# Query and key products of a hybrid GLA/RetNet trunk: three matmuls of 256 columns in two PSUM banks in place of one of 512 and one of 256 in four

## The chip, the cores and the metric

The kernel runs on one core of a Trainium2 chip. TensorE (PE in the profile) multiplies; its weight loads are listed apart, as PEld. VectorE (DVE), ScalarE (ACT) and GpSimd (POOL) do the rest, and SyncE (SP) issues most DMAs. TensorE writes its results to PSUM, eight banks of 128 x 512 float32 values. The metric is the time of one execution on the device, in microseconds (us); lower is better.

## The reference

The model has two layers over a sequence of 256 tokens with 2048 channels: a gated linear attention (GLA, 4 heads) and a retention layer (8 heads). Each normalizes its input, projects it to queries, keys, values and gates, mixes tokens with a decay, normalizes each head, multiplies by `silu(gate)`, projects back and adds the result to its input. What matters here are the projections:

```python
proj = h @ w_in                                   # h: 256 x 2048
q, k, v, gate = jnp.split(proj, [...], axis=-1)
...
return (o * jax.nn.silu(gate)) @ w_out
```

A head has 256 query and 256 key columns, so a head's queries and keys together are one block of 512 columns of `w_in`. All values are float32.

## The kernel before

**Precision.** A float32 product is made of three products of split numbers. Every weight block and every activation is split into a high part, rounded to the matmul's format, and a low part, the rest. High by high, high by low and low by high are summed in PSUM. The activations lie in `xhl`: for each of 16 rows of channel tiles (`kt`), the high and the low copy of all 256 tokens side by side, 512 columns.

**Weights.** They stream from HBM in pieces of 128 x 2 x 512 (512 KB), called subs here. `emit_split` makes a sub's high part on ScalarE (L283) and its low part on VectorE (L284). `next_weights` runs three subs ahead of TensorE (`LOOK`), with four buffers for each part. DMAs run up to six subs ahead (`DMA_LOOK`) in eight buffers. The list of subs, and so the order of loads, is made by `_plan`.

**Values and gates** have tokens as PSUM rows: the weight that TensorE holds is a tile of activations, and 512 weight columns stream past (`group_x`, `product`, `direct`). One bank holds 128 tokens. Most of these products go through a scheme with seven products in place of eight (Strassen's kind) over half of the channels: `P1` to `P8` are half products over summed activations or summed weights, `v4` to `g7` are plain steps. Weight sums are made partly by DMAs that add into a loaded piece (`emit_split`, L292, on GpSimd's queue) and partly on VectorE (L278). `values_and_gates` works through a string of such tokens with four banks, A, B, C and V1: A and B end as the gates, C and V1 as the values. `UNIT` is the order of a GLA pair, `WHOLE` that of retention heads 0 and 4 (eight q/k steps first), and `MIXED` that of the other six retention heads, in which q/k steps stand between the products.

**Queries and keys** have channels as PSUM rows, since the scores need them so: TensorE holds a 128 x 128 tile of weights, and tokens stream past. `step_w` does this for one sub: 2 rows of tiles (`q`) by 4 column blocks (`c`). For each, the high weights meet high and low tokens in one matmul of 512 columns, which fills a whole bank (`ps[c]`, half for high tokens, half for low), and the low weights meet the high tokens in one of 256 columns, which adds to the first half. A head has eight such steps, and four banks for its four column blocks: two of the ring of four (`acc`), and two of the pool `lev`; GLA head 0 has four of the ring. At the end the two halves of each bank are added: ScalarE copies the second half out, and VectorE adds the first (`evac_w` for GLA, `qk_done` for retention).

**Order.** `acc` hands the ring's banks out in turn, unless it is told which. Small work of a head (rotary angles, scores, norms, transposes) is a generator that advances by one step after each token (`advance`, `step`, `turn`). In `ret_head`, `drain` names the token at which all of the last head's small work must be done and that of this head is queued. Within these dependencies a scheduler sets each engine's final order.

Of the kernel before, what the change touches and what calls it, by code (L numbers as in the profile page):

```python
# [10 lines left out]
F32 = mybir.dt.float32  # L11
# [3 lines left out]
AF = mybir.ActivationFunctionType  # L15
ALU = mybir.AluOpType

P = 128
SEQ = 256
D = 2048  # L20
EPS = 1e-6
NKT = D // P
GW = 512
SUB = 2
NSUB = NKT // SUB
# [113 lines left out]


UNIT = "P1 v4 z P3 v5 P5 v6 P6 P2 v7 P7 g4 g5 P8 g6 g7"
MIXED = "q0 q1 P1 q2 q3 q4 z P5 q5 P6 q6 q7 P2 P3 v4 v5 v6 P7 v7 g4 g5 P8 g6 g7"
WHOLE = " ".join(f"q{j}" for j in range(NSUB)) + " " + UNIT


# [16 lines left out]
def kernel(  # L162
# [17 lines left out]
    nc = tc.nc  # L180
# [9 lines left out]
    t4_p = pool("t4", 4)  # L190
# [150 lines left out]

    def step_w(rhs, ps, j, given=True, early=False):
        hi, lo = next_weights()
        last = j == NSUB - 1
        order = [(q, c) for q in range(SUB) for c in range(4)]
        if last or (j == 0 and given):
            order = [(q, c) for c in range(4) for q in range(SUB)]
        if early:
            for q in range(SUB):
                kt = j * SUB + q  # L350
                for c in range(4):
                    keep(mm(ps[c], hi[:, q, c * P : (c + 1) * P], rhs[:, kt, :, :], start=kt == 0, stop=False))
                for c in range(4):
                    keep(mm(ps[c][:, 0, :], lo[:, q, c * P : (c + 1) * P], rhs[:, kt, 0, :], start=False, stop=False))
            order = []
        for q, c in order:
            kt = j * SUB + q
            wh = hi[:, q, c * P : (c + 1) * P]
            wl = lo[:, q, c * P : (c + 1) * P]
            if kt == NKT - 1:  # L360
                mm(ps[c][:, 0, :], wl, rhs[:, kt, 0, :], start=False, stop=False)
                mm(ps[c], wh, rhs[:, kt, :, :], start=False, stop=True)
            else:
                mm(ps[c], wh, rhs[:, kt, :, :], start=kt == 0, stop=False)  # L364
                mm(ps[c][:, 0, :], wl, rhs[:, kt, 0, :], start=False, stop=False)  # L365

    def group_w(rhs, name, extra=None, ps=None):
        given = ps is not None
        ps = ps or acc(4, f"{name}_ps", (P, 2, SEQ))
        for j in range(NSUB):  # L370
            step_w(rhs, ps, j, given, j < 3 and extra is not None and not given)
            if extra is not None:
                extra(j)
            advance()
        return ps

    def evac_w(ps, dst, name):
        tmp = t4_p.tile([P, 4, SEQ], F32, tag="t4", name=f"{name}_h2")
        with tc.high_priority():
            for c in range(4):  # L380
                nc.scalar.activation(tmp[:, c, :], ps[c][:, 1, :], AF.Copy)
                halves = lambda a: a.rearrange("p (z t) -> p z t", z=2)
                to = dst[:, c // 2, :].rearrange("p (z k t) -> p z k t", z=2, k=2)[:, :, c % 2, :]
                nc.vector.tensor_tensor(to, halves(ps[c][:, 0, :]), halves(tmp[:, c, :]), ALU.add)

    begun, closed = set(), set()

# [420 lines left out]
    def gla_head(h):  # L808
        hw = {}
        if h > 1:  # L810
            side.appendleft(gla_decay(h, hw))
        banks = None
        if h > 0:
            banks = acc(2, f"gqk{h}_ps", (P, 2, SEQ))
            banks += [lev_p.tile([P, 2, SEQ], F32, tag="lev", name=f"gqk{h}_ps{c}") for c in (2, 3)]
        ps = group_w(xhl, f"gqk{h}", None if h else first_group, banks)
        drain_side()

        def scores():
            yield from gla_scores(h, hw)  # L820

        qk = t4_p.tile([P, 2, 2 * SEQ], F32, tag="qk", name=f"qk{h}", bufs=1)
        evac_w(ps, qk, f"gqk{h}")
        hw["qk"] = qk
        if h == 0:
            side.append(gate_low_rank())
# [412 lines left out]
    def ret_head(h):  # L1239
        lhs = xhl  # L1240
        mixed = h % 4 != 0
        at = (2, 3, 0, 1) if h < 4 else (0, 1, 2, 3)
        q_ps = [acc(1, f"rqk{h}_ps{c}", (P, 2, SEQ), [at[c + 2]])[0] for c in range(2)]
        q_ps += [lev_p.tile([P, 2, SEQ], F32, tag="lev", name=f"rqk{h}_ps{c}") for c in (2, 3)]
        if not mixed:
            q_ps = q_ps[2:] + q_ps[:2]
        r, r2 = r2_[:, 0, :], r2_[:, 1, :]
        box = {}

        def qk_done():  # L1250
            if h == 0:
                token_norm(r2_, "n2")
                nc.vector.tensor_tensor(r2_[:, 1, :], r2_[:, 0, :], r2_[:, 0, :], ALU.mult)
            qk = t4_p.tile([P, 4, SEQ], F32, tag="qk", name=f"rqk{h}", bufs=1)
            tmp = t4_p.tile([P, 4, SEQ], F32, tag="t4", name=f"rqk{h}_h2")
            for c in range(4):
                nc.scalar.activation(tmp[:, c, :], q_ps[c][:, 1, :], AF.Copy)
                nc.vector.tensor_tensor(qk[:, c, :], q_ps[c][:, 0, :], tmp[:, c, :], ALU.add)
            box["qk"] = qk

        def q_step(j):
            step_w(lhs, q_ps, j)
            if j == NSUB - 1:
                qk_done()

        def tile_of(key, pool_, shape, dtype, name):
            def get():
                if key not in box:
                    box[key] = pool_.tile(shape, dtype, tag=key, name=name)
                return box[key]  # L1270

            return get

        v = tile_of("v", v_p, [P, 2, 2, GW], F32R, f"rv{h}")
        sg = tile_of("sg", sg_p, [P, 2, GW], F32, f"rsg{h}")
        o = tile_of("o", o_p, [P, 2, GW], F32, f"re{h}")
        order = ret_order(h)
        toks = [x for x in order.split() if x != "z"]
        drain = toks.index("P2" if mixed else "v5")

        def turn(tok):
            n = toks.index(tok)
            if n == drain:
                while tasks:
                    step()
                if mixed:
                    tasks.append(ret_tasks(h, box["qk"], r, r2, box))
            elif n < drain:
                if tok != "q7":
                    step()  # L1290
            elif mixed:
                if tok not in ("P7", "g4", "g5"):
                    step()
            elif tok == "P8":
                tasks.append(ret_tasks(h, box["qk"], r, r2, box))
            elif tok in ("g6", "g7"):
                step()

        def banks(n):
            if n not in box:  # L1300
                box[n] = acc(1, f"re{h}_ps{n}", which=[at[n]])[0]
            return box[n]

        values_and_gates(lhs, order, banks, v, sg, o, r, r2, turn, q_step)

    def values_and_gates(lhs, order, banks, v, sg, o, r, r2, turn, q_step=None):
# [5 lines left out]
        tt = nc.vector.tensor_tensor  # L1312
        copy = lambda dst, ps: nc.scalar.activation(dst, ps, AF.Copy)
        done = set()

        def v_split(t):
            sc = r2[:, t : t + 1]
# [5 lines left out]
        def g_done(t):  # L1323
# [7 lines left out]
            "P1": lambda: product(A(), plain(0, 0), stop=True),  # L1331
            "P2": lambda: product(B(), plain(4, 0)),
            "P3": lambda: product(C(), summed(0)),
            "P5": lambda: product(B(), summed(1), stop=True),
            "P6": lambda: product(A(), summed(2), stop=True),
            "P7": lambda: product(A(), summed(3), stop=True),
            "P8": lambda: product(A(), plain(4, 1)),
# [1 line left out]
        for tok in order.split():  # L1339
            kind, last = tok[0], tok[1:] == str(NSUB - 1)  # L1340
            if tok == "z":
                continue
            if kind == "q":
                q_step(int(tok[1:]))
            elif kind == "P":
                products[tok]()
            else:
                direct(lhs, (C(), V1()) if kind == "v" else (B(), A()), int(tok[1:]), stop=last)
            done.add(tok)
            if tok == "P1":  # L1350
                copy(sg()[:, 0, :], A())
            elif tok == "P5":
                copy(o()[:, 1, :], B())
                begun.discard(id(B()))
                closed.discard(id(B()))
            elif tok == "P6":
                copy(o()[:, 0, :], A())
                tt(o()[:, 0, :], o()[:, 1, :], o()[:, 0, :], ALU.subtract)
            elif tok == "P7":
                copy(sg()[:, 1, :], A())  # L1360
                tt(o()[:, 1, :], o()[:, 1, :], sg()[:, 1, :], ALU.subtract)
            if tok in ("v7", "P7"):
                if tok == "v7":
                    tt(o()[:, 0, :], C(), o()[:, 0, :], ALU.add)
                    v_split(0)
                if {"v7", "P7"} <= done:
                    tt(o()[:, 1, :], V1(), o()[:, 1, :], ALU.add)
                    v_split(1)
            if tok == "g7":
                for t in range(2):  # L1370
                    g_done(t)
            turn(tok)
# [135 lines left out]
```

## Time and profile before

| | |
|---|---|
| time, three runs | 1379.7, 1380.17, 1381.68 us (median 1380.17) |
| time of the profiled execution | 1379.47 us |
| its span, first to last instruction | 1377.6 us |
| matmul records, weight load records | 6632, 6632 |
| VectorE busy, ScalarE busy | 1079.1, 836.0 us |
| mean granted TensorE clock | 0.998 |

The profile is of one execution. A row of a group reads: line, engine, operation, output<-inputs, shapes, count, then busy time in us and the mean duration of one in ns, then idle time of the engine before them and what ended it. A row of the timeline begins with the start and the duration in us and ends with the idle time before it. Rows of a tile give shortest, median and longest duration in ns, and first and last start in us. Matmuls overlap in their pipeline, and their recorded ends are modelled. A row's mean duration of 390 ns is therefore not what one costs; the distance between starts is. A few matmul records can be missing.

### The profile page before, as it was taken

How to read it: one execution, taken by the hardware profiler on the slowest of the kernel's cores; microseconds unless marked ns; L12 is line 12 of the kernel's file. 1: busy time of each engine (PE TensorE's matmuls, PEld its weight loads, DVE VectorE, ACT ScalarE, POOL GpSimd, SP SyncE). 2: the span in 40 equal slices, each digit the busy share in tenths (PEclk: the TensorE clock that was granted, in tenths of full speed). 3: DMA queues.
4: the chain of work that ended last, by engine and by line, in shares of the span. 5: the costliest groups of instructions: out<-in, count | busy, mean ns of one | idle time of the engine just before them, and what ended most of it. 6: DMA issues, size and time to landing. Idle time of an engine off the chain costs nothing.

```text
span 1377.6 us, 18438 instructions
## 1 busy us (share of the span) xinstructions
PE 1366.5 (99%) x6632; PEld 1148.5 (83%) x6632; DVE 1079.1 (78%) x1497; ACT 836.0 (61%) x1104; POOL 131.8 (10%) x188
## 2 busy tenths in 40 slices
PE   9999999999999999999999999999999999999997
PEld 7888888888888888888888888888888888888887
DVE  6686795987878896769888888886858897888673
ACT  6576656656567747656666566655546666666452
POOL 1003020110021021001011010100101101010000
PEclk9999999999999999999999999999999999999999
DMA  9765556689658657858897878896798797879661
GB/s 359 245 182 160 172 177 187 151 250 343 204 153 265 204 175 180 314 168 247 279 317 202 256 203 247 208 310 206 184 372 238 217 271 193 256 199 327 211 191 62
DMA packets 83931, 312.94 MB, mean 227 GB/s; under 512 B 9712, under 2 KB 10736, under 8 KB 82560
## 3 DMA queue, kind: packets, MB, share of 16 engines
q1 hardware_dynamic: 67344, 242.64, 50.9%
q0 software_dynamic: 15056, 61.74, 22.6%
q10 hardware_dynamic: 1440, 7.38, 1.4%
q8 instruction: 52, 0.85, 0.2%
q14 instruction: 39, 0.32, 0.1%
HBM read 301.24 MB, written 10.49 MB: 226 GB/s over the span
## 4 chain that ended last, share of the span: by engine, by line
PE 99%; DMA 0%; DVE 0%; ACT 0%; DVEq 0%; issue 0%; SPq 0%
PE rqk_ps L364 8%; PE re_ps L392 8%; PE re_ps L391 8%; PE re_ps L393 8%; PE rqk_ps L365 4%; PE gqk_ps L364 4%; PE gg_ps L322 3%; PE gv_ps L321 3%; PE gv_ps L322 3%; PE gv_ps L323 3%; PE gg_ps L323 3%; PE gg_ps L321 3%; PE ge_ps L392 2%; PE ge_ps L393 2%; PE ge_ps L391 2%; PE gae_ps L391 2%
## 5 line engine op out<-in xcount | busy, mean ns | idle before, releaser
L284 DVE TENSOR_TENSOR lo<-raw,hi 128x1024 fp32r<-128x1024 f32 (+1 forms) x557 | 675.2, 1222 | 225.7 <-ACT hi L283 218.9
L283 ACT ACTIVATE hi<-raw 128x1024 fp32r<-128x1024 f32 (+1 forms) x557 | 584.5, 1056 | 390.8 <-PE gg_ps L323 49.0
L364 PE MATMUL rqk_ps<-xhl,hi 128*128 128x512 f32 x480 | 162.8, 397 | 0.0
L392 PE MATMUL re_ps<-lo,xhl 128*128 128x512 f32 x352 | 137.3, 390 | 0.0
L393 PE MATMUL re_ps<-hi,xhl 128*128 128x512 f32 x352 | 137.1, 390 | 0.0
L391 PE MATMUL re_ps<-hi,xhl 128*128 128x512 f32 x352 | 132.7, 391 | 0.0
L292 POOL DMA_DIRECT2D raw<-in_w_all x84 | 72.7, 867 | 530.3 <-DVE lo L284 283.8
L365 PE MATMUL rqk_ps<-xhl,lo 128*128 128x256 f32 x480 | 122.3, 280 | 0.0
L364 PEld LDWEIGHTS rqk_ps<-xhl,hi 128*128 128x128 f32 x480 | 89.5, 188 | 17.9
L365 PEld LDWEIGHTS rqk_ps<-xhl,lo 128*128 128x128 f32 x480 | 87.5, 189 | 3.4
L393 PEld LDWEIGHTS re_ps<-hi,xhl 128*128 128x128 f32 x352 | 66.1, 188 | 13.6
L391 PEld LDWEIGHTS re_ps<-hi,xhl 128*128 128x128 f32 x352 | 66.1, 188 | 13.3
L392 PEld LDWEIGHTS re_ps<-lo,xhl 128*128 128x128 f32 x352 | 66.1, 188 | 13.1
L364 PE MATMUL gqk_ps<-xhl,hi 128*128 128x512 f32 x216 | 76.5, 398 | 0.0
L322 PE MATMUL gg_ps<-lo,xhl 128*128 128x512 f32 x192 | 75.4, 393 | 0.0
L322 PE MATMUL gv_ps<-lo,xhl 128*128 128x512 f32 x192 | 75.2, 392 | 0.0
L321 PE MATMUL gv_ps<-hi,xhl 128*128 128x512 f32 x192 | 75.1, 393 | 0.0
L323 PE MATMUL gv_ps<-hi,xhl 128*128 128x512 f32 x192 | 75.0, 391 | 0.0
L323 PE MATMUL gg_ps<-hi,xhl 128*128 128x512 f32 x192 | 74.9, 390 | 0.0
L321 PE MATMUL gg_ps<-hi,xhl 128*128 128x512 f32 x192 | 74.8, 391 | 0.0
L365 PE MATMUL gqk_ps<-xhl,lo 128*128 128x256 f32 x216 | 59.0, 280 | 0.0
L801 POOL TENSOR_TENSOR s<-s,m 128x64 f32<-128x64 f32 x56 | 36.1, 676 | 232.7 <-DVE m L792 223.4
(407 smaller groups left out, 2682.5 us busy)
## 6 DMA issues: line engine op xcount, KB each, us to landing
raw<-in_w_all SPq DMA_DIRECT2D x451, 512.0 KB, 4.8
raw<-in_w_all POOLq DMA_DIRECT2D x84, 512.0 KB, 6.5
resid<-in_x_n SPq DMA_DIRECT2D x2, 1024.0 KB, 9.1
gg<-in_gn_g POOLq DMA_DIRECT2D x8, 256.0 KB, 3.9
resid_x<-resid ACTq DMA_DIRECT2D x1, 2048.0 KB, 9.1
gb<-in_gn_b POOLq DMA_DIRECT2D x8, 256.0 KB, 6.2
gb_resid<-resid_x POOLq DMA_DIRECT2D x1, 2048.0 KB, 11.8
resid_g<-gb_resid ACTq DMA_DIRECT2D x1, 2048.0 KB, 8.9
```

What stands on the lines that cost most here:

```text
L283: a = nc.scalar.activation(hi[:, sl], src[:, sl], AF.Copy)
L284: b = nc.vector.tensor_tensor(lo[:, sl], src[:, sl], hi[:, sl].bitcast(F32), ALU.subtract)
L292: nc.gpsimd.dma_start(raws[n], block(key), accum_op=ALU.add)
L321: mm(ps, xh, hi[:, q, :], start=kt == 0, stop=False)
L322: mm(ps, xh, lo[:, q, :], start=False, stop=False)
L323: mm(ps, xl, hi[:, q, :], start=False, stop=kt == NKT - 1)
L364: mm(ps[c], wh, rhs[:, kt, :, :], start=kt == 0, stop=False)
L365: mm(ps[c][:, 0, :], wl, rhs[:, kt, 0, :], start=False, stop=False)
L391: mm(ps, xh, hi[:, q, :], start=start, stop=False, **again)
L392: mm(ps, xh, lo[:, q, :], start=False, stop=False, **again)
L393: mm(ps, xl, hi[:, q, :], start=False, stop=stop, **again)
L801: nc.gpsimd.tensor_tensor(dst, dst, side_of(m[:, li, :], z), ALU.add)
```

## The change

The query and key matmuls all have 256 columns now. High weights by high tokens, high weights by low tokens and low weights by high tokens are three matmuls that add into the same 256 columns. So the sum is complete in PSUM, and a bank holds two column blocks. A head needs two banks. GLA heads take them from the ring; retention heads take both from `lev`. The evacuation is one ScalarE copy for each bank, and no VectorE add.

In retention heads the ring's banks are no longer held by queries and keys. In mixed heads, product 5 goes into bank C, the first values' bank, and product 3 adds onto it there. Product 2, which used to come after q7 since product 5 had bank B before it, now comes after q3. The values' first half then takes product 6 off with a subtraction at `v7`, and a subtraction on VectorE after `P6` is dropped. The small work of a mixed head is queued after q7, not after `P2`.

```diff
-MIXED = "q0 q1 P1 q2 q3 q4 z P5 q5 P6 q6 q7 P2 P3 v4 v5 v6 P7 v7 g4 g5 P8 g6 g7"
+MIXED = "q0 q1 P1 q2 q3 P2 q4 z P5 q5 P6 q6 q7 P3 v4 v5 v6 P7 v7 g4 g5 P8 g6 g7"
...
     def step_w(rhs, ps, j, given=True, early=False):
         hi, lo = next_weights()
-        last = j == NSUB - 1
+        at = lambda c: ps[c // 2][:, c % 2, :]
+        both = lambda c: {"skip_group_check": c % 2 == 1}
...
-            if kt == NKT - 1:
-                mm(ps[c][:, 0, :], wl, rhs[:, kt, 0, :], start=False, stop=False)
-                mm(ps[c], wh, rhs[:, kt, :, :], start=False, stop=True)
-            else:
-                mm(ps[c], wh, rhs[:, kt, :, :], start=kt == 0, stop=False)
-                mm(ps[c][:, 0, :], wl, rhs[:, kt, 0, :], start=False, stop=False)
...
+            a = [
+                lambda c=c, wh=wh, kt=kt: mm(at(c), wh, rhs[:, kt, 0, :], start=kt == 0 and c % 2 == 0, stop=False, **both(c)),
+                lambda c=c, wh=wh, kt=kt: mm(at(c), wh, rhs[:, kt, 1, :], start=False, stop=False, **both(c)),
+            ]
+            b = [lambda c=c, wl=wl, kt=kt: mm(at(c), wl, rhs[:, kt, 0, :], start=False, stop=kt == NKT - 1, **both(c))]
+            if not early:
+                for x in a + b:
+                    x()
+                continue
...
+    def group_w(rhs, name, extra=None, given=False):
+        ps = acc(2, f"{name}_ps", (P, 2, SEQ))
...
-    def evac_w(ps, dst, name):
-        tmp = t4_p.tile([P, 4, SEQ], F32, tag="t4", name=f"{name}_h2")
+    def evac_w(ps, dst):
         with tc.high_priority():
-            for c in range(4):
-                nc.scalar.activation(tmp[:, c, :], ps[c][:, 1, :], AF.Copy)
-                halves = lambda a: a.rearrange("p (z t) -> p z t", z=2)
-                to = dst[:, c // 2, :].rearrange("p (z k t) -> p z k t", z=2, k=2)[:, :, c % 2, :]
-                nc.vector.tensor_tensor(to, halves(ps[c][:, 0, :]), halves(tmp[:, c, :]), ALU.add)
+            for i in range(2):
+                to = dst[:, i, :].rearrange("p (z k t) -> p k z t", z=2, k=2)
+                nc.scalar.activation(to, ps[i].rearrange("p k (z t) -> p k z t", z=2), AF.Copy)
...
-        banks = None
-        if h > 0:
-            banks = acc(2, f"gqk{h}_ps", (P, 2, SEQ))
-            banks += [lev_p.tile([P, 2, SEQ], F32, tag="lev", name=f"gqk{h}_ps{c}") for c in (2, 3)]
-        ps = group_w(xhl, f"gqk{h}", None if h else first_group, banks)
+        ps = group_w(xhl, f"gqk{h}", None if h else first_group, h > 0)
...
-        q_ps = [acc(1, f"rqk{h}_ps{c}", (P, 2, SEQ), [at[c + 2]])[0] for c in range(2)]
-        q_ps += [lev_p.tile([P, 2, SEQ], F32, tag="lev", name=f"rqk{h}_ps{c}") for c in (2, 3)]
-        if not mixed:
-            q_ps = q_ps[2:] + q_ps[:2]
+        q_ps = [lev_p.tile([P, 2, SEQ], F32, tag="lev", name=f"rqk{h}_ps{c}") for c in range(2)]
...
-            tmp = t4_p.tile([P, 4, SEQ], F32, tag="t4", name=f"rqk{h}_h2")
-            for c in range(4):
-                nc.scalar.activation(tmp[:, c, :], q_ps[c][:, 1, :], AF.Copy)
-                nc.vector.tensor_tensor(qk[:, c, :], q_ps[c][:, 0, :], tmp[:, c, :], ALU.add)
+            for i in range(2):
+                nc.scalar.activation(qk[:, 2 * i : 2 * i + 2, :], q_ps[i], AF.Copy)
...
-        drain = toks.index("P2" if mixed else "v5")
+        drain = toks.index("q7" if mixed else "v5")
...
+        first = order.index("P5") < min(order.index("P3"), order.index("v4"))
...
-            "P5": lambda: product(B(), summed(1), stop=True),
+            "P5": lambda: product((C if first else B)(), summed(1), stop=True),
...
             elif tok == "P6":
                 copy(o()[:, 0, :], A())
-                tt(o()[:, 0, :], o()[:, 1, :], o()[:, 0, :], ALU.subtract)
+                if not first:
+                    tt(o()[:, 0, :], o()[:, 1, :], o()[:, 0, :], ALU.subtract)
...
-                    tt(o()[:, 0, :], C(), o()[:, 0, :], ALU.add)
+                    tt(o()[:, 0, :], C(), o()[:, 0, :], ALU.subtract if first else ALU.add)
```

Three places of TensorE's order show it. The first is in GLA head 1's queries and keys, in before (`gqk1_ps0` to `gqk1_ps2` are banks of a column block each; `hi41`, `lo41` are the parts of sub 41):

```order
L364 MATMUL gqk1_ps0_1304<-xhl_105,hi41_1215 128x512
L365 MATMUL gqk1_ps0_1304<-xhl_105,lo41_1216 128x256
L364 MATMUL gqk1_ps1_1305<-xhl_105,hi41_1215 128x512
L365 MATMUL gqk1_ps1_1305<-xhl_105,lo41_1216 128x256
L364 MATMUL gqk1_ps2_1306<-xhl_105,hi41_1215 128x512
L365 MATMUL gqk1_ps2_1306<-xhl_105,lo41_1216 128x256
```

and with the change (`gqk1_ps0` and `gqk1_ps1` hold two column blocks each):

```order
L355 MATMUL gqk1_ps0_1359<-xhl_105,hi41_1270 128x256
L356 MATMUL gqk1_ps0_1359<-xhl_105,hi41_1270 128x256
L358 MATMUL gqk1_ps0_1359<-xhl_105,lo41_1271 128x256
L355 MATMUL gqk1_ps1_1360<-xhl_105,hi41_1270 128x256
L356 MATMUL gqk1_ps1_1360<-xhl_105,hi41_1270 128x256
L358 MATMUL gqk1_ps1_1360<-xhl_105,lo41_1271 128x256
```

A pair of widths, 512 and 256, has become three rows of 256 into one place, the first two with the same weights.

The second place is the end of a mixed head's q steps, head 1, in before (`re1_ps10` is bank B, `re1_ps20` bank C, `sums` the summed activations):

```order
L365 MATMUL rqk1_ps3_6351<-xhl_105,lo297_6599 128x256
L361 MATMUL rqk1_ps3_6351<-xhl_105,lo297_6599 128x256
L362 MATMUL rqk1_ps3_6351<-xhl_105,hi297_6598 128x512
L392 MATMUL re1_ps10_6547<-lo298_6611,xhl_105 128x512
L393 MATMUL re1_ps10_6547<-hi298_6610,xhl_105 128x512
L391 MATMUL re1_ps10_6547<-hi298_6610,xhl_105 128x512
L392 MATMUL re1_ps10_6547<-lo298_6611,xhl_105 128x512
L393 MATMUL re1_ps10_6547<-hi298_6610,xhl_105 128x512
```

and with the change:

```order
L355 MATMUL rqk1_ps1_6624<-xhl_105,hi299_6951 128x256
L356 MATMUL rqk1_ps1_6624<-xhl_105,hi299_6951 128x256
L358 MATMUL rqk1_ps1_6624<-xhl_105,lo299_6952 128x256
L390 MATMUL re1_ps20_6887<-hi300_6963,sums_6124 128x512
L391 MATMUL re1_ps20_6887<-lo300_6964,sums_6124 128x512
L392 MATMUL re1_ps20_6887<-hi300_6963,sums_6124 128x512
L390 MATMUL re1_ps20_6887<-hi300_6963,sums_6124 128x512
L391 MATMUL re1_ps20_6887<-lo300_6964,sums_6124 128x512
```

Product 2 stood behind the last q step; now product 3 stands there, and product 2 has moved to behind q3.

The third place is the passage from GLA head 1's last gate group (`gg3_ps1`) to the first output half (`gae0_ps1`), with transposes of head 1's output (`got2_tp`), in before:

```order
L322 MATMUL gg3_ps1_2118<-lo79_2231,xhl_105 128x512
L323 MATMUL gg3_ps1_2118<-hi79_2230,xhl_105 128x512
L679 MATMUL got2_tp0_2267<-ident_103,go2_1984 128x128
L679 MATMUL got2_tp1_2295<-ident_103,go2_1984 128x128
L391 MATMUL gae0_ps1_2326<-hi80_2250,ogt_106 128x512
L679 MATMUL got2_tp0_2267<-ident_103,go2_1984 128x128 x3
L679 MATMUL got2_tp1_2295<-ident_103,go2_1984 128x128 x3
L392 MATMUL gae0_ps1_2326<-lo80_2251,ogt_106 128x512
L393 MATMUL gae0_ps1_2326<-hi80_2250,ogt_106 128x512
```

and with the change:

```order
L322 MATMUL gg3_ps1_2228<-lo79_2341,xhl_105 128x512
L323 MATMUL gg3_ps1_2228<-hi79_2340,xhl_105 128x512
L678 MATMUL got2_tp0_2377<-ident_103,go2_2094 128x128
L678 MATMUL got2_tp1_2405<-ident_103,go2_2094 128x128
L678 MATMUL got2_tp0_2377<-ident_103,go2_2094 128x128 x3
L678 MATMUL got2_tp1_2405<-ident_103,go2_2094 128x128 x3
L390 MATMUL gae0_ps1_2436<-hi80_2360,ogt_106 128x512
L391 MATMUL gae0_ps1_2436<-lo80_2361,ogt_106 128x512
L392 MATMUL gae0_ps1_2436<-hi80_2360,ogt_106 128x512
```

The first output matmul stood among the transposes; now all eight transposes stand ahead of it. It writes the bank that `gg3_ps1` had, since the ring of banks is shifted by two.

More of the change, by code (lines that the diff above doesn't have):

```diff
@@ L343, in step_w @@
         hi, lo = next_weights()
-        last = j == NSUB - 1
+        at = lambda c: ps[c // 2][:, c % 2, :]
+        both = lambda c: {"skip_group_check": c % 2 == 1}
         order = [(q, c) for q in range(SUB) for c in range(4)]
-        if last or (j == 0 and given):
+        if j == NSUB - 1 or (j == 0 and given):
             order = [(q, c) for c in range(4) for q in range(SUB)]
-        if early:
-            for q in range(SUB):
-                kt = j * SUB + q
-                for c in range(4):
-                    keep(mm(ps[c], hi[:, q, c * P : (c + 1) * P], rhs[:, kt, :, :], start=kt == 0, stop=False))
-                for c in range(4):
-                    keep(mm(ps[c][:, 0, :], lo[:, q, c * P : (c + 1) * P], rhs[:, kt, 0, :], start=False, stop=False))
-            order = []
+        his, los = [], []
         for q, c in order:
@@ L359, in step_w @@
             wl = lo[:, q, c * P : (c + 1) * P]
-            if kt == NKT - 1:
-                mm(ps[c][:, 0, :], wl, rhs[:, kt, 0, :], start=False, stop=False)
-                mm(ps[c], wh, rhs[:, kt, :, :], start=False, stop=True)
-            else:
[L364 to L369, printed above, removed]
+            a = [
[7 more added lines that the diff above has]
+                continue
+            his += a
+            los += b
+            if c == 3:
+                for x in his + los:
+                    keep(x())
+                his, los = [], []
+    def group_w(rhs, name, extra=None, given=False):
+        ps = acc(2, f"{name}_ps", (P, 2, SEQ))
         for j in range(NSUB):
@@ L375, in group_w @@
         return ps
-    def evac_w(ps, dst, name):
-        tmp = t4_p.tile([P, 4, SEQ], F32, tag="t4", name=f"{name}_h2")
+    def evac_w(ps, dst):
         with tc.high_priority():
-            for c in range(4):
-                nc.scalar.activation(tmp[:, c, :], ps[c][:, 1, :], AF.Copy)
-                halves = lambda a: a.rearrange("p (z t) -> p z t", z=2)
-                to = dst[:, c // 2, :].rearrange("p (z k t) -> p z k t", z=2, k=2)[:, :, c % 2, :]
-                nc.vector.tensor_tensor(to, halves(ps[c][:, 0, :]), halves(tmp[:, c, :]), ALU.add)
+            for i in range(2):
+                to = dst[:, i, :].rearrange("p (z k t) -> p k z t", z=2, k=2)
+                nc.scalar.activation(to, ps[i].rearrange("p k (z t) -> p k z t", z=2), AF.Copy)
     begun, closed = set(), set()
@@ L822, in gla_head @@
         qk = t4_p.tile([P, 2, 2 * SEQ], F32, tag="qk", name=f"qk{h}", bufs=1)
-        evac_w(ps, qk, f"gqk{h}")
+        evac_w(ps, qk)
         hw["qk"] = qk
@@ L1254, in qk_done @@
             qk = t4_p.tile([P, 4, SEQ], F32, tag="qk", name=f"rqk{h}", bufs=1)
-            tmp = t4_p.tile([P, 4, SEQ], F32, tag="t4", name=f"rqk{h}_h2")
-            for c in range(4):
-                nc.scalar.activation(tmp[:, c, :], q_ps[c][:, 1, :], AF.Copy)
-                nc.vector.tensor_tensor(qk[:, c, :], q_ps[c][:, 0, :], tmp[:, c, :], ALU.add)
+            for i in range(2):
+                nc.scalar.activation(qk[:, 2 * i : 2 * i + 2, :], q_ps[i], AF.Copy)
             box["qk"] = qk
@@ L1352, in values_and_gates @@
             elif tok == "P5":
-                copy(o()[:, 1, :], B())
-                begun.discard(id(B()))
-                closed.discard(id(B()))
+                copy(o()[:, 1, :], (C if first else B)())
+                if not first:
+                    begun.discard(id(B()))
+                    closed.discard(id(B()))
             elif tok == "P6":
                 copy(o()[:, 0, :], A())
-                tt(o()[:, 0, :], o()[:, 1, :], o()[:, 0, :], ALU.subtract)
+                if not first:
+                    tt(o()[:, 0, :], o()[:, 1, :], o()[:, 0, :], ALU.subtract)
             elif tok == "P7":
```

## The prediction

> **What bounds the kernel now.** I read the page's first lines, then the waits of TensorE, then its busy time by stage.
>
> ```profile
> span 1377.6 us, 18438 instructions
> PE 1366.5 (99%) x6632; PEld 1148.5 (83%) x6632; DVE 1079.1 (78%) x1497; ACT 836.0 (61%) x1104; POOL 131.8 (10%) x188
> PE 99%; DMA 0%; DVE 0%; ACT 0%; DVEq 0%; issue 0%; SPq 0%
> PE warm_ps L505 <- POOL warm L503: 1.8, 1, 1.8
> PE gqk_ps L352 <- ACT hi L283: 1.3, 1, 1.3
> 16.00:640.00 624.00, 624.00 (x2976) 522.33 (x2975) 484.57 (x705) 389.02 (x516) 65.41 (x92) 1.00 0.70 212
> 640.00:1333.00 693.00, 693.00 (x3364) 582.56 (x3364) 565.64 (x738) 421.65 (x543) 62.39 (x82) 1.00 0.83 247
> ```
>
> The third row is the chain of waits, the next two are all that TensorE (PE) waited for, and the last two are stages (length, then busy time of PE, PEld, DVE, ACT, POOL, then granted clock, DMA share, GB/s). TensorE waits for others only at the very start, 3.1 us in all, and from 16 to 1333 us it is busy all the time at a granted clock of 1.00. VectorE (DVE) and ScalarE (ACT) have room, at 78% and 61%. But a busy matmul overlaps its neighbours, so these rows do not say what one costs. So the question is what the instructions of the edited groups cost TensorE from start to start. Whatever is taken from the other engines is worth nothing while that holds.
>
> **What a matmul costs.** Three rows of time give it: a stretch of 30 matmuls of 512 columns before the tail, the tail, whose matmuls have 256 columns, and alternating q/k matmuls.
>
> ```profile
> 1339.70 0.39 PE L321 MATMUL rb_ps<-hi,ogt 128*128 128x512 f32 x1
> ...
> 1346.27 0.39 PE L323 MATMUL rb_ps<-hi,ogt 128*128 128x512 f32 x1
> L322 PE MATMUL tail_ps<-tail,ogt x64: 278/283/283, 1346.5 to 1369.2; 128*128 128x256 f32 x64
> L323 PE MATMUL tail_ps<-xhl,ogt x64: 279/283/283, 1346.6 to 1369.3; 128*128 128x256 f32 x64
> 1014.69 0.40 PE L364 MATMUL rqk_ps<-xhl,hi 128*128 128x512 f32 x1
> 1014.92 0.28 PE L365 MATMUL rqk_ps<-xhl,lo 128*128 128x256 f32 x1
> 1015.04 0.40 PE L364 MATMUL rqk_ps<-xhl,hi 128*128 128x512 f32 x1
> ...
> 1015.75 0.40 PE L364 MATMUL rqk_ps<-xhl,hi 128*128 128x512 f32 x1
> ```
>
> 512 columns: (1346.27 - 1339.70) / 29 = 226.6 ns. 256 columns: from the first L322 to the last L323 of the tail there are 191 matmuls, 64 + 64 and 63 of L321, so (1369.3 - 1346.5) / 190 = 120.0 ns. The difference, 106.6 ns, buys 256 columns; so 226.6 - 2 x 106.6 = 13.4 ns of each matmul is a fixed part, whatever its width. Three alternating pairs (1014.69 to 1015.75) take 1.06 us, 353.3 ns a pair. That is 6.7 ns over 226.6 + 120.0: changing widths at every instruction has a small price of its own.
>
> **The change, part by part.** *The q/k groups.* Each of 768 pairs (12 heads, 16 rows of tiles, 4 column blocks) becomes three matmuls of 256 columns. The columns stay 768; one instruction with its fixed part is added. The new stream is uniform, and the tail is the same form, three in a row into one PSUM place with a load of weights each: 3 x 120.0 = 360.0 ns. In the order of before, 508 of the 768 short matmuls stand between two long ones, and 260 stand in blocks of equal width. At 353.3 and at 346.6 ns the mean pair is (508 x 353.3 + 260 x 346.6) / 768 = 351.0 ns. So each pair loses 9.0 ns, and 768 pairs lose 6.9 us. Bounds: were all pairs at 353.3, 6.7 x 768 = 5.1 us; were all at 346.6, 13.4 x 768 = 10.3 us. Off that come some 0.2 us for the first head's earliest pairs:
>
> ```profile
> 5.62 2.07 PE L352 MATMUL gqk_ps<-xhl,hi 128*128 128x512 f32 x4 [1.30 <-ACT hi L283]
> 7.49 1.05 PE L354 MATMUL gqk_ps<-xhl,lo 128*128 128x256 f32 x4
> 8.35 1.91 PE L352 MATMUL gqk_ps<-xhl,hi 128*128 128x512 f32 x4
> ```
>
> Here four short ones take 8.35 - 7.49 = 0.86 us, 215 ns each, twice the 106.6 ns that their columns take later: no fixed part is to be seen, and none is lost. Some 20 pairs lie there.
>
> The same weights now stand twice in a row (high columns against high and low tokens). Before has such repeats already, in the value and gate groups, where L321 and L322 share their weights:
>
> ```profile
> L322 PEld LDWEIGHTS gg_ps<-lo,xhl 128*128 128x128 f32 x192 | 36.1, 188 | 7.4 <-issue 0.2
> L321 PEld LDWEIGHTS gg_ps<-hi,xhl 128*128 128x128 f32 x192 | 36.0, 188 | 7.3
> ```
>
> Both are loaded 192 times, and the L321/L322/L323 stretch above keeps 226.6 ns throughout: a repeat saves nothing.
>
> The Trainium skill, "TensorE: Matmul & The Clock Gate", section "Wait — 56ns, not 53.3ns?", puts the fixed part of a warm matmul at about 2.5 ns. By that the sum would be 2.5 x 768 = 1.9 us. The rows above, 226.6 and 120.0 ns in this kernel, differ from it, and the sum goes by the rows.
>
> *The evacuations.* Each head gives up four half-width copies on ScalarE and four adds on VectorE, and gets two full-width copies.
>
> ```profile
> L1258 DVE TENSOR_TENSOR rqk<-rqk_ps,rqk_h 128x256 f32<-128x256 f32 x32 | 12.4, 419 | 0.2
> L384 DVE TENSOR_TENSOR qk<-gqk_ps,gqk_h 128x256 f32<-128x256 f32 x16 | 6.0, 418 | 0.2
> L1257 ACT ACTIVATE rqk_h<-rqk_ps 128x256 f32<-128x256 f32 x32 | 12.3, 384 | 6.6 <-PE rqk_ps L362 5.8
> L1313 ACT ACTIVATE re<-re_ps 128x512 f32<-128x512 f32 x16 | 9.5, 596 | 3.8 <-PE re_ps L393 3.7
> L1358 DVE TENSOR_TENSOR re<-re x8: 683/686/693, 699.3 to 1239.7; 128x512 f32<-128x512 f32 x8
> ```
>
> VectorE loses 12.4 + 6.0 us, and 6 x 0.69 us for the subtraction that the mixed heads drop: 22.5 us. ScalarE loses 48 x 0.384 and gains 24 x 0.596: 4.1 us. Neither ends a wait of TensorE after the start, so this counts as nothing. If that cover were gone it would be a gain, bounded by what TensorE idles, and after the start that is a few tenths.
>
> *Product 2 earlier, product 5 in the first values' bank, tasks drained at q7.* No matmul is added. What can change is when DMAs come due. In mixed heads one transfer is already on the brink, the accumulating DMA that product 3's split issues on POOL's queue and product 7 needs:
>
> ```profile
> 822.02 0.85 POOL L292 DMA_DIRECT2D raw<-in_w_all  x1 [8.33 <-DMA raw<-in_w_all]
> 825.38 0.85 POOL L292 DMA_DIRECT2D raw<-in_w_all  x1 [2.51 <-DVE lo L284]
> 835.04 2.01 ACT L283 ACTIVATE hi<-raw 128x1024 fp32r<-128x1024 f32 x2 [4.45 <-DMA raw<-in_w_all]
> 837.11 0.39 PE L391 MATMUL re_ps<-hi,sums 128*128 128x512 f32 x1
> 837.41 0.50 PE L392 MATMUL re_ps<-lo,sums 128*128 128x512 f32 x1
> 837.74 0.39 PE L393 MATMUL re_ps<-hi,sums 128*128 128x512 f32 x1
> ```
>
> Issued at 825.38, it lets ScalarE go on at 835.04, 9.7 us later; the matmul at 837.41 is some 0.07 us late, the next 0.10 more. With product 2 gone from between q7 and product 3, the splits of product 3 have the longer q6 and q7 ahead of them instead of product 2's short steps. Four weight buffers let a split run when the step four before it is done; with 6 matmuls a half product (1.36 us) and 8 triples a q step (2.88 us) the second split moves from 3 x 1.36 = 4.1 us before its use to 2 x 2.88 + 1.36 = 7.1 us. Product 1's accumulating DMAs get product 2's 2.7 us more until product 5. Product 5's copy out of the shared bank has q5, product 6, q6 and q7, over 11 us, before product 3 writes there. Gain: 0 to 0.5 us; I take 0.2.
>
> *Banks.* Head 0's group now takes two banks of the ring, not four, which shifts every pair of banks up to the first output half. There the last gate group's second bank becomes that of the output's first product.
>
> ```profile
> 250.35 1.39 ACT L659 ACTIVATE gsg<-gg_ps,rr 128x512 f32<-128x512 f32 x2 [0.98 <-PE gg_ps L323]
> 250.84 0.38 PE L679 MATMUL got_tp<-ident,go 128*128 128x128 f32 x2
> 250.97 0.48 PE L391 MATMUL gae_ps<-hi,ogt 128*128 128x512 f32 x1
> 251.29 0.82 PE L679 MATMUL got_tp<-ident,go 128*128 128x128 f32 x6
> 251.87 0.48 PE L392 MATMUL gae_ps<-lo,ogt 128*128 128x512 f32 x1
> ```
>
> The SiLU pair frees the bank at 250.35 + 1.39 = 251.74; the output's first matmul ran at 250.97 in before. Now eight transposes go first, and six took 0.58 us (251.29 to 251.87), so TensorE would be there near 251.6. Cost 0.1 to 0.4 us, once; I take 0.2. Behind it on TensorE stands all the rest, so it counts in full.
>
> Sum: 6.9 - 0.2 - 0.2 + 0.2 = +6.7 us on the profiled execution's 1379.47, hence 1386.2. The median of the three runs shown, 1380.17, is 0.7 above that execution, so I expect **1386.9 us**, 0.5% slower.
>
> **The rivals.** *New waits in the mixed heads, slower still.* For it: the 9.7 us of the accumulating DMA against a lead of that size, and a DMA share of 0.83 in the stage of 640 to 1333 us. Product 2's two loads now come before those that product 6 adds in; if these arrived a load late, six heads would stall. It decides from where a head's slack of a few tenths is used up; at 1 us a head it gives 6 more, 1393. Against it: the same loads are taken away after q7, where the only late transfer stands.
>
> *A repeated weight tile is cheap, not slower.* If the second of two matmuls with the same weights went without its fixed part, the triple would cost 226.6 + 120.0 = 346.6 ns, 4.4 less than the mean pair: 768 x 4.4 = 3.4 us gained, 1376.8. It decides once the repeat costs under 120.0 - 9.0 = 111.0 ns. Against it: the L321/L322 rows.
>
> *The extra matmul's fixed part is mostly hidden, no change.* With half of the 13.4 ns gone, a triple costs 353.3 ns, 2.3 more than the mean pair: +1.8 us, 1382.0. For it: a short matmul behind a long one starts the next 0.12 us later or less (1014.92 to 1015.04). Against it: the tail, 120.0 ns over 191 matmuls. The 2.5 ns of the Trainium skill's section named above would end close by, at 1380.17 + 1.9 = 1382.1; no row here shows it.
>
> *The scheduler undoes the edit.* Excluded: the changed order has 2304 q/k matmuls of 256 columns, three for each pair, in two banks a head.
>
> **How the numbers follow.** Forecast 0.86; new waits 0.08; cheap repeats 0.03; a hidden fixed part 0.03. Within 0.2% (2.8 us, about what a measurement of this kernel can tell from no change) lies the last, with 0.01 of a forecast that falls short: same 0.04. Faster 0.03. Slower 0.85 + 0.08 = 0.93. The forecast's bounds, 5.1 and 10.3 with -0.6 and +0.4 from the small terms, run from 1384.7 to 1390.9; I give 1384.5 to 1390.9 and leave the rest of the rivals out.
>
> **What would show it.** After: 768 more matmuls; TensorE still 99% busy, its waits the same two rows; q/k matmuls starting every 120 ns; the 64 triples of an unmixed head 23.0 us long, where 64 pairs at 353.3 ns take 22.6; VectorE down by some 22 us. Wrong if q/k matmuls start less than 117 ns apart, or if TensorE shows waits of over 1 us after 16 us.

## The result, and the profile after

The changed kernel takes 1387.14 us (median of four runs, 1386.39 to 1388.39); before took 1380.93 us beside it (four runs, 1379.7 to 1381.72). The ratio is 1.0049, with a 95% interval of 1.0037 to 1.0061: the change makes the kernel slower by half a per cent. The forecast was 1386.9 us, in a range of 1384.5 to 1390.9.

The page of the changed kernel and its list of TensorE's waits answer the first rows shown of before:

```profile
span 1385.1 us, 19893 instructions
PE 1373.7 (99%) x7400; PEld 1190.4 (86%) x7400; DVE 1061.5 (77%) x1443; ACT 833.1 (60%) x1080; POOL 133.0 (10%) x188
PE warm_ps L504 <- POOL warm L502: 1.8, 1, 1.8
PE gqk_ps L355 <- ACT hi L283: 1.3, 1, 1.3
PE gbe_ps L391 <- DVE lo L284: 0.3, 1, 0.3
```

The span is 7.5 us longer, and TensorE has 768 records more (7400 against 6632). Its waits are the two of the start, with one of 0.3 us added. So the time did not go into waiting. It went into the matmuls themselves: TensorE's busy time grew by 7.2 us. The timeline and the tile's rows show retention head 4, whose q/k steps stand alone:

```profile
1016.34 0.28 PE L356 MATMUL rqk_ps<-xhl,hi 128*128 128x256 f32 x1
1016.46 0.28 PE L358 MATMUL rqk_ps<-xhl,lo 128*128 128x256 f32 x1
1016.58 0.28 PE L355 MATMUL rqk_ps<-xhl,hi 128*128 128x256 f32 x1
...
L356 PE MATMUL rqk_ps<-xhl,hi x64: 277/283/283, 1016.3 to 1039.0; 128*128 128x256 f32 x64
L358 PE MATMUL rqk_ps<-xhl,lo x64: 282/283/283, 1016.5 to 1039.1; 128*128 128x256 f32 x64
L355 PE MATMUL rqk_ps<-xhl,hi x63: 283/283/283, 1016.6 to 1038.9; 128*128 128x256 f32 x63
```

The 191 matmuls of these rows start 120.0 ns apart ((1039.1 - 1016.3) / 190). The 64 triples take 23.0 us where the pairs of before took 353.3 ns each, 22.6 us. The 283 ns of a row is longer than the 120 ns from start to start, since matmuls overlap, so it says nothing about that.

At the passage from GLA head 1 to the first output half, the timeline of ScalarE and TensorE shows the wait for the bank that the forecast named:

```profile
250.90 1.37 ACT L658 ACTIVATE gsg<-gg_ps,rr 128x512 f32<-128x512 f32 x2 [0.98 <-PE gg_ps L323]
251.39 1.03 PE L678 MATMUL got_tp<-ident,go 128*128 128x128 f32 x8
252.33 0.50 PE L390 MATMUL gae_ps<-hi,ogt 128*128 128x512 f32 x1
```

The SiLU pair ends at 252.27, and the output's first matmul starts 0.06 us behind it. Eight transposes take 0.94 us here; six took 0.58 in before, so at that pace eight would have been done by 252.16. By that estimate the bank costs some 0.2 us.

In the mixed heads the accumulating DMA is no longer at the brink. This is GpSimd's, ScalarE's and TensorE's timeline in head 2:

```profile
825.38 0.86 POOL L292 DMA_DIRECT2D raw<-in_w_all  x1 [4.20 <-DVE lo L284]
827.38 0.85 POOL L292 DMA_DIRECT2D raw<-in_w_all  x1 [1.15 <-DVE lo L284]
832.81 1.06 ACT L283 ACTIVATE hi<-raw 128x1024 fp32r<-128x1024 f32 x1 [0.48 <-DMA raw<-in_w_all]
836.43 1.06 ACT L283 ACTIVATE hi<-raw 128x1024 fp32r<-128x1024 f32 x1 [2.56 <-DMA raw<-in_w_all]
840.58 0.39 PE L390 MATMUL re_ps<-hi,sums 128*128 128x512 f32 x1
840.80 0.39 PE L391 MATMUL re_ps<-lo,sums 128*128 128x512 f32 x1
...
841.94 0.39 PE L390 MATMUL re_ps<-hi,sums 128*128 128x512 f32 x1
```

Product 7 starts at 840.58, and its second sub, whose transfer is the late one, six matmuls later, at 841.94. ScalarE still waits for that transfer, but goes on at 836.43, and the low part made behind it is needed at 842.16, 5.7 us later. In before ScalarE went on at 835.04 for a matmul at 837.41, 2.4 us later. So the transfer gained some 3 us of room, as the prediction had it. The pace there is now 0.23 us throughout.

### The profile page after: what moved, and what is told of

It is laid out like the page before. It is cut to its first block, busy times and chain, and to the rows that moved or that the text cites. A ratio compares the mean times of both kernels' runs of the same rounds, so it can differ in the third digit from the quotient of the medians.

```text
span 1385.1 us, 19893 instructions
## 1 busy us (share of the span) xinstructions
PE 1373.7 (99%) x7400; PEld 1190.4 (86%) x7400; DVE 1061.5 (77%) x1443; ACT 833.1 (60%) x1080; POOL 133.0 (10%) x188
## 4 chain that ended last, share of the span: by engine, by line
PE 97%; DMA 1%; DVE 1%; ACT 0%; issue 0%; DVEq 0%; SPq 0%; ACTq 0%
PE re_ps L390 8%; PE re_ps L391 8%; PE re_ps L392 8%; PE rqk_ps L358 4%; PE rqk_ps L356 4%; PE rqk_ps L355 4%; PE gg_ps L322 3%; PE gv_ps L323 3%; PE gv_ps L321 3%; PE gv_ps L322 3%; PE gg_ps L323 3%; PE gg_ps L321 3%; PE gqk_ps L355 2%; PE gqk_ps L356 2%; PE gqk_ps L358 2%; PE ge_ps L392 2%
## 5 line engine op out<-in xcount | busy, mean ns | idle before, releaser
L355 PE MATMUL rqk_ps<-xhl,hi 128*128 128x256 f32 x512 | 144.6, 284 | 0.0
L356 PE MATMUL rqk_ps<-xhl,hi 128*128 128x256 f32 x512 | 144.2, 283 | 0.0
L358 PE MATMUL rqk_ps<-xhl,lo 128*128 128x256 f32 x512 | 141.6, 283 | 0.0
L355 PEld LDWEIGHTS rqk_ps<-xhl,hi 128*128 128x128 f32 x512 | 97.9, 191 | 1.7
L356 PEld LDWEIGHTS rqk_ps<-xhl,hi 128*128 128x128 f32 x512 | 98.0, 191 | 1.4
L358 PEld LDWEIGHTS rqk_ps<-xhl,lo 128*128 128x128 f32 x512 | 96.6, 192 | 0.4
L390 PEld LDWEIGHTS re_ps<-hi,xhl 128*128 128x128 f32 x352 | 66.1, 188 | 13.1
L355 PE MATMUL gqk_ps<-xhl,hi 128*128 128x256 f32 x256 | 73.2, 289 | 1.3 <-ACT hi L283 1.3
```

Source lines behind the costliest of these rows:

```text
L355: lambda c=c, wh=wh, kt=kt: mm(at(c), wh, rhs[:, kt, 0, :], start=kt == 0 and c % 2 == 0, stop=False, **both(c)),
L356: lambda c=c, wh=wh, kt=kt: mm(at(c), wh, rhs[:, kt, 1, :], start=False, stop=False, **both(c)),
L358: b = [lambda c=c, wl=wl, kt=kt: mm(at(c), wl, rhs[:, kt, 0, :], start=False, stop=kt == NKT - 1, **both(c))]
L390: mm(ps, xh, hi[:, q, :], start=start, stop=False, **again)
```

## The experiments

Each run has before beside it on the same chip. The first four share a before of 1379.84 us (nine runs), the last three one of 1380.54 us (fifteen runs). All kernels compute the whole model.

### Only the triples (e1_triples_only)

```diff
...
-                mm(ps[c], wh, rhs[:, kt, :, :], start=kt == 0, stop=False)
-                mm(ps[c][:, 0, :], wl, rhs[:, kt, 0, :], start=False, stop=False)
+                for a in range(2):
+                    mm(ps[c][:, a, :], wh, rhs[:, kt, a, :], start=kt == 0 and a == 0, stop=False, skip_group_check=True)
+                mm(ps[c][:, 0, :], wl, rhs[:, kt, 0, :], start=False, stop=False, skip_group_check=True)
```

> Before, with each q/k pair of 512 and 256 columns split into three matmuls of 256 columns; the four banks, the copies and adds, and the order of the tokens stay as in before. Theory (each matmul has a fixed part of 13.4 ns, and a change of width costs some 6.7 ns): 768 more matmuls cost 6.9 us, less 0.2 us at the slow start, so +6.7 us on before, 1387.6 us at a before of 1380.9; q/k matmuls start every 120 ns; VectorE keeps its 1079 us. Rival (the changed kernel lost its time by its new banks, evacuation or token order): within 1 us of before.

Measured: 1387.93 us, ratio 1.0056 (1.0042 to 1.0070), 8.1 us over before, by the interval 5.8 to 9.7; the expected 6.7 lies within. The profiled execution's span is 9.1 us longer. The page has VectorE's work as before, and the timeline the new pace:

```profile
PE 1374.4 (99%) x7400; PEld 1190.4 (86%) x7400; DVE 1080.0 (78%) x1497; ACT 836.2 (60%) x1104; POOL 132.1 (10%) x188
1017.88 0.28 PE L368 MATMUL rqk_ps<-xhl,lo 128*128 128x256 f32 x1
1018.00 0.40 PE L367 MATMUL rqk_ps<-xhl,hi 128*128 128x256 f32 x2
1018.24 0.28 PE L368 MATMUL rqk_ps<-xhl,lo 128*128 128x256 f32 x1
```

Three matmuls take 0.36 us here too (1017.88 to 1018.24). The new banks, the new evacuation and the new token order are all absent, and the time is that of the change, with overlapping intervals. So the split of the wide matmul makes the loss. The 1080.0 us of VectorE, against the change's 1061.5, buy or cost nothing that these runs can tell.

### The change with the old mixed heads (e2_old_mixed)

```diff
-MIXED = "q0 q1 P1 q2 q3 P2 q4 z P5 q5 P6 q6 q7 P3 v4 v5 v6 P7 v7 g4 g5 P8 g6 g7"
+MIXED = "q0 q1 P1 q2 q3 q4 z P5 q5 P6 q6 q7 P2 P3 v4 v5 v6 P7 v7 g4 g5 P8 g6 g7"
...
-        drain = toks.index("q7" if mixed else "v5")
+        drain = toks.index("P2" if mixed else "v5")
...
-        first = order.index("P5") < min(order.index("P3"), order.index("v4"))
+        first = False
```

> The change without its part in the mixed heads: product 2 behind q7 again, product 5 in bank B, the subtraction after product 6, small work queued after product 2; q/k matmuls and evacuation as in the change. Theory: the moved products cost and gain nothing that TensorE sees, so the time is that of the change within 0.6 us, +6.0 to +6.8 us on before. Rival (the mixed heads' order brings new waits that the change pays for): over 1 us faster than the change. Rival (it hides what the q/k part costs): over 1 us slower.

Measured: 1387.07 us, ratio 1.0050 (1.0036 to 1.0064), against the change's 1387.14 and 1.0049. That is 7.2 us over the before beside it, a little over the 6.0 to 6.8 expected, but with an interval of 5.0 to 8.8. The moved products are worth nothing in time that these runs can tell. The 3 us of room that the transfer of product 7 gained, seen above, was room where TensorE had lost some 0.2 us in head 2 (0.07 and 0.10 in the prediction's rows).

### No weights twice in a row (e4_apart)

```diff
-                for x in a + b:
+                for x in (a[0], b[0], a[1]) if kt < NKT - 1 else (a[0], a[1], b[0]):
                     x()
```

> The change with the three matmuls of a triple in another order: high weights by high tokens, low weights, high weights by low tokens, so that no weights stand twice in a row. Theory (a repeated weight tile saves nothing): as the change, within 0.5 us. Rival (a repeat saves half of its fixed part of 13.4 ns): 768 x 6.7 = 5 us slower than the change; and one nanosecond saved by each repeat would show as 0.8 us.

Measured: 1386.94 us, ratio 1.0053 (1.0040 to 1.0065). The medians alone can't tell differences of under a microsecond, but the trace can: its matmuls too start 0.12 us apart (1019.00, 1019.12, 1019.24, 1019.36), repeated weights or not. Both pages list as many weight loads as matmuls, 7400 of each. So a repeated weight tile is loaded again here, and saves nothing.

### Widths in strict blocks (e3_blocks)

```diff
...
+                for f in (narrow, wide) if last else (wide, narrow):
+                    for c in cs:
+                        for q in range(SUB):
+                            keep(f(q, c))
...
```

`wide` is the matmul of 512 columns, `narrow` that of 256; `keep` binds an instruction to the order in which the program lists it.

> Before with the same matmuls of 512 and 256 columns, but in each q/k step all eight of 512 columns first, then all eight of 256 (by column block in the last step). The places where a 512 follows a 256 fall from 637 to 145. Theory (a change of width costs 6.7 ns a cycle, the excess of 353.3 over 346.6 ns): 492 x 6.7 = 3.3 us less than before, 1377.6 us at a before of 1380.9. Rival (the 6.7 ns are no price of changing widths, but of this stream's own, as of adding low weights' products into half of a bank): no change, within 0.7 us of before.

Measured: 1409.73 us, ratio 1.0214 (1.0200 to 1.0228), 30 us over before: neither expectation. The list of TensorE's waits has eleven entries, of which the largest are

```profile
PE re_ps L406 <- ACT hi L283: 6.6, 4, 1.7
PE got_tp L694 <- issue: 5.6, 1, 5.6
PE re_ps L407 <- DVE lo L284: 4.3, 4, 1.4
```

All eleven come to 25.6 us, against 3.1 in before. Behind the longest of them the timeline has

```profile
140.87 3.71 PE L356 MATMUL gqk_ps<-xhl,hi 128*128 128x512 f32 x8
144.42 1.12 PE L360 MATMUL gqk_ps<-xhl,lo 128*128 128x256 f32 x8
```

Eight wide matmuls take 3.55 us, 0.44 us each, twice the usual time: the granted clock was 0.50 from 138 to 141 us and 0.58 from 141 to 145. So the wait of 5.6 us cost more than itself. The next run has the same blocks without the binding and none of these long waits, so the binding makes the loss; which other bound work TensorE waited for was not traced. The run tells nothing about widths.

### The same blocks, not bound (e6_blocks_free)

Against the kernel of the run above:

```diff
-                            keep(f(q, c))
+                            f(q, c)
```

> Before with each q/k step's eight matmuls of 512 columns ahead of its eight of 256, as in the blocks before, but with the scheduler free to move them among other work. Places where a 512 follows a 256: 152, not 637. Theory (a change of width costs 6.7 ns a cycle): 485 x 6.7 = 3.2 us less than before, 1376.7 us at a before of 1379.9; between 2 and 4 us less. Rival (the 6.7 ns belong to adding low weights' products, not to the width): within 0.7 us of before. Rival (the order of the strict blocks was itself bad for TensorE, not its binding to other work): 10 us or more slower.

Measured: 1377.88 us, ratio 0.9983 (0.9974 to 0.9992), 2.7 us under before, by the interval 1.1 to 3.6, and as expected; the span is 1.5 us shorter. It is faster than both kernels. The timeline of head 4 shows the steps:

```profile
1015.16 1.12 PE L360 MATMUL rqk_ps<-xhl,lo 128*128 128x256 f32 x8
1016.12 2.00 PE L356 MATMUL rqk_ps<-xhl,hi 128*128 128x512 f32 x8
1017.96 1.11 PE L360 MATMUL rqk_ps<-xhl,lo 128*128 128x256 f32 x8
```

Eight narrow matmuls take 0.96 us (1015.16 to 1016.12), 120 ns each. Eight wide ones take 1.84 us, 230 ns each and not 226.6. A step of eight pairs takes 2.80 us, 350 ns a pair, against 353.3 when widths alternate. So alternating has a price, as expected. But it is not the same for each change of width: a cycle (a change of width and back) costs in blocks 2.80 - 8 x 0.3466 = 0.03 us, more than one of 6.7 ns. Over the 96 steps of all heads, 0.026 us a step (350 against 353.3 ns a pair) would be 2.5 us, an estimate that head 4's pace gives. So the gain comes from there being fewer cycles, 152 and not 637, though each of them is dearer.

### Another group's matmuls split (e5_halves_x)

```diff
-                    mm3(ps[t], lhs, j * SUB + q, t, hi, lo, q)
+                    halves3(ps[t], lhs, j * SUB + q, t, hi, lo, q)
```

`halves3` makes the three products of `mm3` in two halves of 256 columns each.

> Before with the matmuls of 512 columns in the plain value, gate and output groups (not the seven-product ones) split into two of 256 each; q/k as in before. 1824 matmuls more, the same columns. Theory (13.4 ns for each matmul whatever group it is in): 1824 x 13.4 = 24.4 us more than before, 1404.3 us at 1379.9; these matmuls start every 120 ns. Rival (the price belongs to the form of the q/k groups, where tokens stream past weights): under half of that, 12 us. By the fixed part of about 2.5 ns that the Trainium skill gives (TensorE: Matmul & The Clock Gate, section Wait - 56ns, not 53.3ns?) it would be 4.6 us.

Measured: 1402.87 us, ratio 1.0161 (1.0147 to 1.0175), 22.3 us over before, by the interval 20.3 to 24.2; the span grew by 23.9 us. In a value group the timeline has

```profile
224.14 0.64 PE L331 MATMUL gv_ps<-hi,xhl 128*128 128x256 f32 x4
224.62 0.40 PE L331 MATMUL gv_ps<-lo,xhl 128*128 128x256 f32 x2
224.86 0.64 PE L331 MATMUL gv_ps<-hi,xhl 128*128 128x256 f32 x4
```

Six start in 0.72 us, again 120 ns each. A split costs 22.3 / 1824 = 12.2 ns by the runs and 13.1 by the spans. The price is thus one of a matmul as such at these two widths, not of the form of the q/k groups. The expected 24.4 us lies just outside of the interval: 13.4 ns is some tenth too much. The Trainium skill's 2.5 ns ("TensorE: Matmul & The Clock Gate", section "Wait — 56ns, not 53.3ns?") gives an estimate of 4.6 us; these runs do not agree with it for this kernel's matmuls.

### Below 256 columns (e8_lo_quarters)

```diff
-            b = [lambda c=c, wl=wl, kt=kt: mm(at(c), wl, rhs[:, kt, 0, :], start=False, stop=kt == NKT - 1, **both(c))]
+            b = [
+                lambda c=c, wl=wl, kt=kt, n=n: mm(
+                    at(c)[:, n : n + P], wl, rhs[:, kt, 0, n : n + P], start=False, stop=kt == NKT - 1, skip_group_check=True
+                )
+                for n in (0, P)
+            ]
...
```

> The change with the low weights' matmul of 256 columns split into two of 128, but for the last row of tiles: 720 matmuls more, the same columns. Theory, if the fixed part of 13.4 ns holds below 256 columns too: 720 x 13.4 = 9.6 us more than the change, 1396.7 us. Rival (below 256 columns a matmul cannot start before its weights are loaded, as the rows of 128 columns in before suggest, 12 in 1.25 us or 104 ns each, though of another kind): 2 x 104 - 120 = 88 ns a split, 63 us more than the change, some 1450 us.

Measured: 1459.99 us, ratio 1.0577 (1.0562 to 1.0591), 73 us over the change, 101 ns for each of 720 splits. The theory of 9.6 us fails; the rival, with 63, comes near. The timeline shows what repeats:

```profile
1070.15 0.28 PE L356 MATMUL rqk_ps<-xhl,hi 128*128 128x256 f32 x1
1070.27 0.34 PE L359 MATMUL rqk_ps<-xhl,lo 128*128 128x128 f32 x2
1070.44 0.33 PE L355 MATMUL rqk_ps<-xhl,hi 128*128 128x256 f32 x1
1070.61 0.28 PE L356 MATMUL rqk_ps<-xhl,hi 128*128 128x256 f32 x1
```

Four matmuls take 0.46 us (1070.15 to 1070.61), 115 ns each, though two of them have 128 columns only. At columns and 13.4 ns they would take 0.37 us. So the sum that holds at 512 and at 256 columns does not hold with 128 mixed in. In this stream the four average 115 ns; the twelve matmuls of 128 columns that the expectation names took 104 ns each, so 115 is no floor for every matmul. That the load of the weights sets the pace fits, since each matmul has one (8120 of each on the page), but no run took the load away.

## Why the prediction was right

**What bounds the kernel.** "Whatever is taken from the other engines is worth nothing while that holds": the change takes 24 us of VectorE instructions away (48 adds of 0.42 us and six subtractions of 0.69) and is slower, and e1 keeps them and takes the same time within what the runs can tell. VectorE's busy time fell by 17.6 us, not by the 22.5 foretold, and ScalarE's by 2.9, not 4.1. Busy time counts overlapping rows once, which would explain a smaller fall; it was not traced further.

**The price of the added matmul.** The step was 768 pairs at 360.0 - 351.0 ns, +6.9 us. The 360.0 ns stand in the rows of the change and of e1 (three times 120.0). The whole came out at +6.2 us by the medians and +7.5 by the spans. The term was rightly sized, within what the runs can tell, and e1 shows that it is the cause. The prediction called the 13.4 ns a part of each matmul "whatever its width". Two widths can't show that, and e8 shows that it fails with 128 columns; the change only needed 512 and 256. What the 13.4 ns consist of stays open.

**The alternation of widths** made the difference between 10.3 and 6.9 us. The mean pair was worked out as if a narrow matmul between two wide ones paid 6.7 ns, and one in a block nothing. e6 shows that blocks pay too, some 0.03 us a cycle. The 351.0 ns was a fair mean, but the rule behind it was too simple. Priced by all 637 places where a 512 follows a 256, as the expectations of e3 and e6 count them, in place of 508, the term would have been 768 x 13.4 ns less 637 x 6.7 ns, 6.0 us and not 6.9. The measured times, 6.2 to 8.1 us over before in the change, e1, e2 and e4, can't tell the two apart. The forecast of +6.7 us met +6.2 on a before that was 0.8 us slower than the one it started from. So that it came within 0.3 us of the median is in part luck.

**Repeated weights.** The rival of cheap repeats, and with it that of a hidden fixed part, falls by e4 and by the pace of 120.0 ns.

**Product 2, product 5 and the banks.** Taken as -0.2 and +0.2 us. The bank's wait was there, by estimate some 0.2 us, and so was the room for the accumulating DMA. e2 shows no difference in time, and terms of 0.2 us are below what the runs can tell. The rival of new waits in the mixed heads did not come about.

**What was not foreseen** is a wait of 0.3 us in the second output half (the third row of TensorE's waits). ScalarE's split ahead of that low part had waited 3.24 us for a transfer, until 642.98. Waits for low parts stand at other places in other kernels here: 0.3, 0.3 and 0.2 us in e1, 0.7 in two places in e2, 0.5 in e4. What sets each of them off stays open.

## What to carry to other kernels

Where TensorE works without a pause, count its instructions as well as its columns: here each matmul of 512 or 256 columns cost 13.4 ns beside its columns by the traces (12.2 by e5's times), each split of 256 into two of 128 cost 101 ns (e8), and splitting 512 into two of 256 bought nothing that paid for it. Work that leaves an engine with slack is worth nothing by itself, however many microseconds it is. Where matmuls of two widths must mix, put them in blocks (2.7 us gained in e6), but leave the scheduler free to move the blocks among other work (32 us between e3 and e6).

## What the runs showed of the hardware

- Columns and a fixed part give the pace at 512 and at 256 columns (226.6 and 120.0 ns), but not with 128 mixed in: in e8 two of 128 and two of 256 columns took 0.46 us together, where the sum gives 0.37.
- A matmul with the weights of the one before it loads them again: as many weight loads as matmuls in the change and in e4 (7400), and 120 ns from start to start in both.
- After an idle stretch TensorE ran slower for some microseconds: in e3, behind a wait of 5.6 us, at a granted clock of 0.50 and 0.58 for 7 us.
- Wide matmuls behind a block of narrow ones are slower for a while: eight of them took 230 ns each in e6, against 226.6 in a long stretch. The cause is open; no run isolated it.
